# Three edits to a fused decoder layer: conditioning loads in column halves, an interleaved PSUM layout, and the order of splits at the start of the expert stage

## The chip, the cores and the metric

The kernel runs on one core of a Trainium2 chip. The metric is the device time of one execution in microseconds (us), taken on the device. The engines are named as in the profile: PE is TensorE (matmul) and PEld its weight loads, DVE is VectorE, ACT is ScalarE, POOL is GpSimd, SP is SyncE, which here only issues DMAs. Before the change three runs took 3036.16, 3039.43 and 3045.69 us; the median is 3039.43 us.

## The reference, cut to what matters

One decoder layer over 1024 tokens of width 1024, in float32. A conditioning vector gives six modulation rows; the attention half uses two kinds of heads; the second half is a retrieval layer over 128 x 128 single-neuron experts.

```python
mod = silu(c) @ ada_w + ada_b                       # 6 rows of 1024: sh1, sc1, g1, sh2, sc2, g2
h = rms_norm(x) * (1 + sc1) + sh1
...                                                 # projections, two kinds of causal attention
x = x + g1 * (mixed @ w_out)
h2 = rms_norm(x) * (1 + sc2) + sh2
s = (h2 @ w_q) . sub_keys                           # 8 heads x 2 halves x 128 scores
sv, si = top_k(s, 16)                               # per half; then the best 16 of 16 x 16 sums
g = softmax(best 16 sums); eidx = expert numbers
a = gelu(u_tab[eidx] . h2)
x = x + g2 * sum((g * a) * v_tab[eidx])
```

## The kernel before, in words

**Stages.** The program is a trunk followed by the expert stage. The trunk's order on each engine is made by a planner that simulates a timeline with costs of its own; the expert stage is in the order in which the code writes it. The trunk runs `ada(0)` (the first third of the conditioning matmul), then `project` woven with `ada_rest` (the other two thirds, `ada(1)` and `ada(2)`), then `block(0, 5)` for the first five token tiles of 128, then `block(5, 3)` for the other three woven with `route_dense`, which turns the routing of the first five tiles into dense gate matrices. `experts` then computes the first five tiles densely (all 128 x 128 experts, by two large matmuls `mm_u` and `mm_v`) and the last three by gathering rows (`gathered`), spread between the dense steps.

**`ada(g, wp)`, lines 181 to 203.** Each third has 2048 columns, four quarters of 512 that go to four 32-partition groups of one PSUM bank (`tile_position=(0, 32*q)`). For g = 0 one DMA of 1 MB brings all four quarters of a 128-row slice `k`. For g = 1 and 2 a DMA of 512 KB brings two quarters (1024 neighbouring columns, 4 KB runs), and the matmuls of these two follow; so 16 DMAs for each g, through two buffers, on the SP queue. One f32 matmul of the program is two PE instructions in the profile, each with a weight load.

**`route_dense`, `matrix(t)`, lines 870 to 907.** For every token tile 32 steps, each for four tokens: DVE compares `A` (four 128 x 128 one-hot matrices), POOL, ACT or DVE make the four `B` (by the letters in `SHARE`), PE multiplies each pair into one fourth of a bank `pg`, and ACT copies the bank into `gs` (line 904). Before the change each product has 128 neighbouring columns of PSUM, and ACT's copy writes every element 128 bytes from the one before, because `gs` has 32 tokens innermost. While `block(5, 3)` is in `attend` there is one `pg` bank, later there are two (`PG`). `A` and `B` have three buffers each, which come free when the products are done.

**`experts`, lines 1002 to 1203.** A step j of 128 does `mm_u(j)` (48 matmuls of 320 columns into the one `mm` bank pair), `gelu(j)` on ACT, `weigh(j)` on DVE, `split_c(j)` (ACT makes `CH`, DVE makes `CL`). Four steps are a group; from step 4 on, each step also runs the `mm_v` blocks of the group before, 12 matmuls each, which need the four `CH`, `CL` of that group and four units of the second table (`vh` by ACT, `vl` by DVE or POOL, in `split_v`). `mm_u(j)` needs units 2j and 2j+1 of the first table (`split_u`: `uh` on ACT, `ul` on DVE or POOL). Units below `UP` and `VP` have their second half on POOL, the others on DVE. Each split also issues the DMA of a later unit on SP. `step()` advances `gathered`: 18 routing pieces of the sixth tile on DVE, which end with its expert numbers `ei`, then a DVE dot product per gathered row; POOL issues the gathers in advance, seven buffers deep.

**The seam** is the start of `experts`. Before the change the order there is: step 0 `mm_u(0)`, `split_u(3)`, ten routing pieces, `gelu(0)`; steps 1 to 3 `mm_u(j)`, `split_u(2j+2)`, `gelu(j)`, `weigh` and `split_c` of the step before, and then `split_u(2j+3)`; in step 3 also `split_v(0)` and `split_v(1)` at the end; step 4 `mm_u(4)`, `split_c(2)`, `split_c(3)`, `split_v(2)`, `split_v(3)`, then the first `mm_v` block.

Of the kernel before, what the change touches and what calls it, by code (L numbers as in the profile page):

```python
# [43 lines left out]
UP, VP = 8, 8  # L44
# [41 lines left out]
def decoder_layer(ctx: ExitStack, tc: tile.TileContext, a, out):  # L86
# [35 lines left out]
    def tpt():  # L122
        return tp.tile([P, 4, P], FT, name="tp")
# [57 lines left out]
    def ada(g, wp):  # L181

        bt = wp.tile([P, 512], FT, name="abias", bufs=1)
        for q in range(4):
            o = a["ada_b"].offset + g * 2048 + q * 512
            (nc.gpsimd if g else nc.scalar).dma_start(bt[32 * q:32 * q + 32, :],
                                bass.AP(tensor=a["ada_b"].tensor, offset=o, ap=[[0, 32], [1, 512]]))
        ps = bank()
        n = 2 if g else 4
        for k in range(8):  # L190
            for q0 in range(0, 4, n):
                w = wp.tile([P, n, 512], FT, name="adaw")
                c = g * 2048 + q0 * 512
                (nc.sync if g or k % 2 == 0 else nc.scalar).dma_start(w, adaw[k, :, c:c + n * 512])
                for q in range(q0, q0 + n):
                    nc.tensor.matmul(ps[32 * q:32 * q + 32, :512], silb[:, k, :], w[:, q - q0, :], start=(k == 0),
                                     stop=(k == 7), skip_group_check=True, tile_position=(0, 32 * q))
        m = bt
        nc.vector.tensor_add(m, ps[:, :512], bt)
        for q in range(4 if g else 0):  # L200
            o = q * 512
            nc.gpsimd.dma_start(modd[2 * g + o // D, o % D:o % D + 512], m[32 * q:32 * q + 1, :])
        return m
# [661 lines left out]
    def route_dense(ts):  # L865

        with ExitStack() as c1:
            rp = pool(c1, "rp", 1)
            gp = pool(c1, "gp", 2)
            def matrix(t):  # L870
# [10 lines left out]
                for b in range(P // GB):  # L881
                    gs = gp.tile([P, P, GB], FT, name="gs")
                    for m0 in range(0, GB, 4):
# [17 lines left out]
                        pg = bank("pg").rearrange("p (a b) -> p a b", b=P) if "pg" in PS else tpt()  # L901
                        for o in range(4):
                            nc.tensor.matmul(pg[:, o, :], A[:, o, :], B[:, o, :], start=True, stop=True)  # L903
                        nc.scalar.activation(gs[:, :, m0:m0 + 4].rearrange("p j t -> p t j"), pg, AF.Copy)  # L904
# [97 lines left out]
    def experts():  # L1002
        with ExitStack() as c1, tc.manual_schedule():
# [42 lines left out]
            def split_v(n):  # L1046
                if n < 2 * P:
# [89 lines left out]
            for j in range(P + NJ):  # L1137
# [19 lines left out]
                if j == 0:  # L1157
                    split_u(3)
                    for _ in range(10):
                        prog[0] = next(sg)  # L1160
# [25 lines left out]
                if not blocks and live:  # L1186

# [105 lines left out]
```

## Time and profile before

| | |
|---|---|
| median of three runs | 3039.43 us |
| the profiled execution | 3038.61 us |
| its span, first to last instruction | 3036.8 us |
| mean granted TensorE clock | 0.974 of full speed |
| busy shares of the span | PE 93%, DVE 85%, POOL 47%, ACT 39% |
| trunk, up to the last copy into `gs` | 0 to 1213 us |
| seam, until the matmuls run without gaps | 1213 to 1274 us |
| dense steps | 1274 to 3037 us |

A row of the timeline has start and length in us, engine, line, operation, what is written and read, a count where neighbours are merged, and in brackets the idle time before it and what ended that. A row of a group has the count, total busy time in us and the mean of one in ns, then the engine's idle time before these instructions and what ended it. [...] The chain of work is followed back from the end; its shares say which lines lay on it in a stretch, and "issue" is time for which it names no cause.

### The profile page before, as it was taken

The page shows a single profiled execution, that of the slowest core. Times are in us where ns is not written, and L with a number is a line of the kernel's source. Part 1 is how long each engine was busy: PE and PEld are TensorE (multiplying, and loading weights), DVE is VectorE, ACT ScalarE, POOL GpSimd, SP SyncE. Part 2 cuts the span into 40 slices and gives each one's busy share as a digit, 9 for nine tenths or more (in the row PEclk, how much of TensorE's full clock was granted, in tenths as well). Part 3 has the DMA queues.
Part 4 walks back from the last instruction along what each step waited for, and adds up shares of the span by engine and source line. Part 5 has one row for each costly group of instructions (what it writes and reads, how often), then busy time and mean ns, then how long its engine had stood idle before and what let it go on. Part 6 is the DMA issues. An engine that isn't in the chain of part 4 may idle for free.

```text
span 3036.8 us, 46727 instructions
## 1 busy us (share of the span) xinstructions
PE 2837.1 (93%) x16323; PEld 2526.6 (83%) x16323; DVE 2570.6 (85%) x5380; ACT 1185.2 (39%) x2371; POOL 1418.7 (47%) x1194
## 2 busy tenths in 40 slices
PE   5999989897888799699999999999999999999998
PEld 3678777796776698699999999999989989998887
DVE  3767366599988899788888999999999999989997
ACT  4554375242886898222322222222222222222221
POOL 1121000000669974343444655566656666655761
PEclk9999999998999899899999999999999999999999
DMA  7664464721445664678798999899999999998995
GB/s 269 201 190 123 134 199 148 277 64 56 126 129 180 210 206 140 224 263 276 255 321 310 321 332 327 319 351 368 361 351 365 358 371 359 361 373 312 365 366 200
DMA packets 375564, 794.22 MB, mean 262 GB/s; under 512 B 31392, under 2 KB 171040, under 8 KB 368672
## 3 DMA queue, kind: packets, MB, share of 16 engines
q0 software_dynamic: 114400, 417.15, 38.3%
q1 hardware_dynamic: 153344, 312.48, 29.5%
q10 hardware_dynamic: 107584, 61.61, 6.9%
q8 instruction: 128, 2.10, 0.3%
q14 instruction: 108, 0.88, 0.1%
HBM read 707.74 MB, written 83.38 MB: 261 GB/s over the span
## 4 chain that ended last, share of the span: by engine, by line
PE 49%; DVE 18%; issue 12%; POOL 7%; DMA 6%; ACT 4%; SPq 0%; DVEq 0%; POOLq 0%; ACTq 0%
PE mm L1063 14%; PE pj L288 4%; PE pj L289 4%; PE pj L290 4%; POOL gath L954 4%; DVE yr L987 4%; DVE gath L974 3%; PE pg L903 3%; PE tp L289 2%; PE tp L290 2%; PE tp L288 2%; POOL B L892 2%; PE acc L288 1%; PE acc L289 1%; PE acc L290 1%
## 5 line engine op out<-in xcount | busy, mean ns | idle before, releaser
L1063 PE MATMUL mm<-h2d,uh 128*128 128x320 f32 x4096 | 770.6, 310 | 10.2 <-ACT C L1070 5.1
L954 POOL DMA_INDIRECT gath<-in_peer_u,ei x384 | 485.5, 1264 | 405.3 <-DVE gath L974 269.4
L1063 PEld LDWEIGHTS mm<-h2d,uh 128*128 128x128 f32 x4096 | 649.7, 189 | 21.1 <-ACT C L1070 6.2
L954 POOL DMA_INDIRECT gath<-in_peer_v,ef x384 | 514.9, 1341 | 307.2 <-DVE yr L987 168.7
L987 DVE SCALAR_TENSOR_TENSOR yr<-gath,co,yr 128x1024 f32<-128x1024 f32 x381 | 487.5, 1280 | 5.5 <-DMA gath<-in_peer_v,ef 1.1
L974 DVE SCALAR_TENSOR_TENSOR gath<-gath,h 128x1024 f32<-128x1024 f32 x384 | 462.7, 1221 | 26.0 <-DMA h<-h2d 13.4
L1063 PE MATMUL mm<-h2d,ul 128*128 128x320 f32 x2048 | 471.2, 311 | 12.9 <-DVE ul L279 12.4
L1070 ACT ACTIVATE C<-mm 128x640 f32<-128x640 f32 x128 | 90.5, 707 | 864.1 <-PE mm L1063 859.0
L892 POOL TENSOR_SCALAR B<-iota,T 128x128 f32<-128x128 f32 x240 | 265.6, 1115 | 266.5 <-DVE T L877 200.7
L1063 PEld LDWEIGHTS mm<-h2d,ul 128*128 128x128 f32 x2048 | 343.0, 188 | 18.3 <-DVE ul L279 17.9
L289 PE MATMUL tp<-vl,CH 128*128 128x512 f32 x600 | 235.6, 393 | 14.8 <-POOL vl L279 11.7
L903 PE MATMUL pg<-B,A 128*128 128x128 f32 x1280 | 197.2, 298 | 48.2 <-POOL B L892 26.8
L278 ACT ACTIVATE vh<-vr 128x512 fp32r<-128x512 f32 x256 | 152.9, 622 | 224.0 <-PE tp L290 145.5
L288 PE MATMUL tp<-vh,CH 128*128 128x512 f32 x600 | 234.6, 391 | 0.0
L290 PE MATMUL tp<-vh,CL 128*128 128x512 f32 x600 | 234.1, 390 | 0.0
L903 PEld LDWEIGHTS pg<-B,A 128*128 128x128 f32 x1280 | 174.9, 206 | 69.0 <-POOL B L892 39.3
L904 ACT ACTIVATE gs<-pg 128x512 f32<-128x512 f32 x160 | 173.8, 1087 | 56.7 <-PE pg L903 56.2
L278 ACT ACTIVATE uh<-ur 128x512 fp32r<-128x512 f32 x256 | 155.4, 619 | 74.8 <-DMA ur<-in_u_t 67.7
L279 DVE TENSOR_TENSOR ul<-ur,uh 128x512 fp32r<-128x512 f32 x248 | 173.6, 700 | 0.0
L279 DVE TENSOR_TENSOR vl<-vr,vh 128x512 fp32r<-128x512 f32 x248 | 160.0, 682 | 7.2 <-ACT vh L278 7.0
L1074 DVE TENSOR_TENSOR C<-C,G 128x640 f32<-128x640 f32 x128 | 105.2, 823 | 55.0 <-ACT C L1070 54.9
L288 PE MATMUL acc<-vh,CH 128*128 128x512 f32 x384 | 149.8, 390 | 0.0
(321 smaller groups left out, 5978.9 us busy)
## 6 DMA issues: line engine op xcount, KB each, us to landing
ur<-in_u_t SPq DMA_DIRECT2D x256, 256.0 KB, 6.3
vr<-in_peer_v SPq DMA_DIRECT2D x256, 256.0 KB, 6.9
gd<-gs ACTq DMA_DIRECT2D x20, 2048.0 KB, 9.3
G<-gd SPq DMA_DIRECT2D x32, 1280.0 KB, 8.8
adaw<-in_ada_w SPq DMA_DIRECT2D x32, 512.0 KB, 4.3
wraw<-in_peer_w_q SPq DMA_DIRECT2D x128, 128.0 KB, 2.7
wraw<-in_w_out SPq DMA_DIRECT2D x32, 256.0 KB, 3.6
wraw<-in_w_in SPq DMA_DIRECT2D x24, 256.0 KB, 3.8
```

Of the source, the lines that this page charges most:

```text
L278: nc.scalar.activation(hi, src, AF.Copy)
L279: (eng or nc.vector).tensor_sub(lo, src, hi.bitcast(FT))
L288: nc.tensor.matmul(out, ah, bh, start=start, stop=False)
L289: nc.tensor.matmul(out, ah, bl, start=False, stop=False)
L290: nc.tensor.matmul(out, al, bh, start=False, stop=stop)
L892: nc.gpsimd.tensor_scalar(B[:, m, :], iota128, T[:, 1, c + m:c + m + 1], T[:, 2, c + m:c + m + 1], op0=OP.is_equal, op1=OP.mult)
L903: nc.tensor.matmul(pg[:, o, :], A[:, o, :], B[:, o, :], start=True, stop=True)
L904: nc.scalar.activation(gs[:, :, m0:m0 + 4].rearrange("p j t -> p t j"), pg, AF.Copy)
L954: nc.gpsimd.indirect_dma_start(out=u, out_offset=None, in_=tab, in_offset=bass.IndirectOffsetOnAxis(ap=idx, axis=0))
L974: nc.vector.scalar_tensor_tensor(got[n], got[n], 1.0, q["h2"], op0=OP.mult, op1=OP.mult, accum_out=q["dots"][:, s:s + 1])
L987: nc.vector.scalar_tensor_tensor(yr, v, q["co"][:, s:s + 1], yr, op0=OP.mult, op1=OP.add)
L1063: nc.tensor.matmul(ps[:, o, 0:C2], s[:, k % 4, :], h2[:, mv, k, o * C2:(o + 1) * C2], start=st, stop=(k == 7 and s is l))
```

## The change

`ada`: for g = 1 and 2 a DMA brings half of the columns (256) of all four quarters in place of all columns of two quarters; the size stays 512 KB and the runs become 1 KB. The eight matmuls of a half have 256 columns; each half has a bank of its own and an addition of its own. `matrix`: the product of token o goes to every fourth column of the bank, so that the four tokens lie side by side; ACT's copy then reads the bank in order and writes runs of four neighbouring elements. `experts`: `split_u(2j+3)` of steps 0 to 3 stands directly behind `gelu(j)`, ahead of `weigh` and `split_c`; `split_v(0)` to `split_v(3)` stand behind it in steps 1 and 2 (their later calls find nothing to do); with `VP` at 0 DVE makes `vl` of the first eight units in place of POOL.

```diff
--- before.py
+++ after.py
@@ -41,7 +41,7 @@
 AHEAD = 2
 PG = 2
 LAGV = 2
-UP, VP = 8, 8
+UP, VP = 8, 0
 
 UR, VR = 3, 4
 
@@ -185,18 +185,20 @@
             o = a["ada_b"].offset + g * 2048 + q * 512
             (nc.gpsimd if g else nc.scalar).dma_start(bt[32 * q:32 * q + 32, :],
                                 bass.AP(tensor=a["ada_b"].tensor, offset=o, ap=[[0, 32], [1, 512]]))
-        ps = bank()
-        n = 2 if g else 4
+
+        H = 256 if g else 512
+        pss = [bank() for _ in range(0, 512, H)]
         for k in range(8):
-            for q0 in range(0, 4, n):
-                w = wp.tile([P, n, 512], FT, name="adaw")
-                c = g * 2048 + q0 * 512
-                (nc.sync if g or k % 2 == 0 else nc.scalar).dma_start(w, adaw[k, :, c:c + n * 512])
-                for q in range(q0, q0 + n):
-                    nc.tensor.matmul(ps[32 * q:32 * q + 32, :512], silb[:, k, :], w[:, q - q0, :], start=(k == 0),
-                                     stop=(k == 7), skip_group_check=True, tile_position=(0, 32 * q))
+            for h0 in range(0, 512, H):
+                w = wp.tile([P, 4, H], FT, name="adaw")
+                src = adaw[k, :, g * 2048:(g + 1) * 2048].rearrange("p (q n) -> p q n", n=512)[:, :, h0:h0 + H]
+                (nc.sync if g or k % 2 == 0 else nc.scalar).dma_start(w, src)
+                for q in range(4):
+                    nc.tensor.matmul(pss[h0 // H][32 * q:32 * q + 32, :H], silb[:, k, :], w[:, q, :],
+                                     start=(k == 0), stop=(k == 7), skip_group_check=True, tile_position=(0, 32 * q))
         m = bt
-        nc.vector.tensor_add(m, ps[:, :512], bt)
+        for i, ps in enumerate(pss):
+            nc.vector.tensor_add(m[:, i * H:(i + 1) * H], ps[:, :H], bt[:, i * H:(i + 1) * H])
         for q in range(4 if g else 0):
             o = q * 512
             nc.gpsimd.dma_start(modd[2 * g + o // D, o % D:o % D + 512], m[32 * q:32 * q + 1, :])
@@ -898,10 +900,12 @@
                             else:
                                 nc.vector.tensor_scalar(B[:, m, :], iota128, T[:, 1, c + m:c + m + 1],
                                                         T[:, 2, c + m:c + m + 1], op0=OP.is_equal, op1=OP.mult)
-                        pg = bank("pg").rearrange("p (a b) -> p a b", b=P) if "pg" in PS else tpt()
+
+                        pg = (bank("pg") if "pg" in PS else tpt().rearrange("p a b -> p (a b)")).rearrange(
+                            "p (j t) -> p j t", t=4)
                         for o in range(4):
-                            nc.tensor.matmul(pg[:, o, :], A[:, o, :], B[:, o, :], start=True, stop=True)
-                        nc.scalar.activation(gs[:, :, m0:m0 + 4].rearrange("p j t -> p t j"), pg, AF.Copy)
+                            nc.tensor.matmul(pg[:, :, o], A[:, o, :], B[:, o, :], start=True, stop=True)
+                        nc.scalar.activation(gs[:, :, m0:m0 + 4], pg, AF.Copy)
                         yield 1.2
                     nc.scalar.dma_start(gd[:, :, t * (P // GB) + b].rearrange("p a j t -> p a (j t)"),
                                       gs.rearrange("p (a j) t -> p a (j t)", j=NJ))
@@ -1044,7 +1048,7 @@
                     nc.sync.dma_start(vr[n], vtab[j, :, c * 512:(c + 1) * 512])
 
             def split_v(n):
-                if n < 2 * P:
+                if n in vr:
                     vs[n] = (vp.tile([P, 512], FR, name="vh"), vp.tile([P, 512], FR, name="vl"))
                     split(vr.pop(n), *vs[n], nc.gpsimd if n < VP else None)
                     load_v(n + VR)
@@ -1155,7 +1159,6 @@
                 if live:
                     ps = mm_u(j)
                 if j == 0:
-                    split_u(3)
                     for _ in range(10):
                         prog[0] = next(sg)
                 while pend:
@@ -1184,6 +1187,10 @@
                     pend.append((*blk, pv))
                     step()
                 if not blocks and live:
+                    split_u(2 * j + 3)
+                    if 0 < j < 3:
+                        split_v(2 * j - 2)
+                        split_v(2 * j - 1)
 
                     for i in (j - 1, j) if j == NJ - 1 else (j - 1,):
                         if i >= 0:
```

## Rows read from the trace of the kernel before

**Rows 1.** Windows: busy us of each engine in five stretches of the span.
```profile
50.00:100.00 50.00, 50.00 (x264) 34.34 (x264) 32.59 (x84) 31.57 (x81) 1.51 (x2) 1.00 0.71 227
...
764.00:918.00 154.00, 131.62 (x925) 119.95 (x924) 134.27 (x355) 128.95 (x247) 104.27 (x95) 0.90 0.40 119
918.00:1060.00 142.00, 112.66 (x635) 95.01 (x633) 122.58 (x269) 106.60 (x199) 142.00 (x121) 0.90 0.63 197
1060.00:1213.00 153.00, 142.30 (x993) 135.55 (x991) 149.12 (x584) 132.47 (x288) 98.19 (x108) 0.99 0.59 178
...
1300.00:1700.00 400.00, 400.00 (x2254) 365.67 (x2254) 336.98 (x592) 104.13 (x175) 181.13 (x146) 1.00 0.84 288
```

**Rows 2.** Timeline of PE: conditioning matmuls, four quarters at once, then two.
```profile
31.66 5.38 PE L196 MATMUL pj<-adaw,silb 128*32 128x512 f32 x32 [1.31 <-DMA adaw<-in_ada_w]
...
99.59 1.05 PE L196 MATMUL pj<-adaw,silb 128*32 128x512 f32 x4
```

**Rows 3.** The chain of work from 38 to 215 us, shares by line.
```profile
by line: PE pj L288 8.9%; PE pj L289 8.3%; PE pj L290 8.2%; DMA wraw<-in_w_in 7.3%; DMA qd<-stage 5.5%; PE pj L196 3.9%; DMA adaw<-in_ada_w 3.6%; PE tp L452 2.2%; DVE wl L279 1.1%; issue 1.0%; ACT hf L367 0.9%; ACT wh L278 0.9%; DVE stage L
```

**Rows 4.** DMA issues, 40 to 200 us, and two queues of the whole span (packets, MB, share of 16 engines).
```profile
adaw<-in_ada_w SPq DMA_DIRECT2D x30, 512.0 KB, 4.3
...
q1 hardware_dynamic: 153344, 312.48, 29.5%
q10 hardware_dynamic: 107584, 61.61, 6.9%
```

**Rows 5.** Groups of instructions by form, 764 to 1213 us.
```profile
L903 PE MATMUL pg<-B,A 128*128 128x128 f32 x1280 | 197.2, 298 | 48.2 <-POOL B L892 26.8 <-issue 11.8 <-ACT gs L904 2.7
...
L904 ACT ACTIVATE gs<-pg 128x512 f32<-128x512 f32 x160 | 173.8, 1087 | 56.7 <-PE pg L903 56.2 <-ACT sc L782 0.2
...
L593 ACT ACTIVATE pT<-tp 128x512 f32<-128x512 f32 x25 | 15.0, 603 | 0.0
```

**Rows 6.** Timeline around one gate product, 830 to 835 us.
```profile
830.46 1.06 ACT L904 ACTIVATE gs<-pg 128x512 f32<-128x512 f32 x1 [1.50 <-PE pg L903]
...
831.62 2.05 PE L903 MATMUL pg<-B,A 128*128 128x128 f32 x8 [1.19 <-issue]
```

**Rows 7.** The chain of work, by line: 764 to 918, 918 to 1060, 1060 to 1213 us.
```profile
by line: PE pg L903 25.1%; PE mm L580 14.3%; issue 10.5%; PE ov L659 9.6%; POOL B L892 7.5%; ACT gs L904 6.6%; PE tp L592 3.7%; ACT pT L593 3.0%; ACT p L564 2.5%; ACT L564 2.5%; ACT B L896 2.3%; ACT pd L564 2.2%; ACT B L895 1.8%; ACT L229 1
...
by line: POOL B L892 36.7%; issue 15.3%; PE pg L903 11.3%; PE pj L289 7.4%; POOL wl L279 7.2%; PE pj L290 6.6%; PE pj L288 6.1%; ACT gs L904 1.6%; ACT B L895 1.4%; ACT B L896 1.2%; ACT L846 0.9%; PE tp L739 0.6%; DVE fp L792 0.5%; ACT wh L2
...
by line: DVE B L899 20.5%; DVE A L887 16.8%; PE pg L903 14.3%; DVE si L792 5.9%; DVE top L793 5.1%; DVE sv L791 4.6%; DVE si L795 4.5%; PE pj L290 4.1%; PE mm L1063 3.9%; PE pj L288 3.8%; PE pj L289 3.7%; DVE sv L794 3.4%; ACT gs L904 2.7%;
```

**Rows 8.** Timeline of PE at full clock: one gate product, four contiguous passes.
```profile
849.89 1.11 PE L903 MATMUL pg<-B,A 128*128 128x128 f32 x8
...
1219.85 0.74 PE L1063 MATMUL mm<-h2d,uh 128*128 128x320 f32 x4
```

**Rows 9.** Timeline of PE in the seam: its longest wait.
```profile
1261.62 0.39 PE L288 MATMUL tp<-vh,CH 128*128 128x512 f32 x1
1273.71 0.80 PE L289 MATMUL tp<-vl,CH 128*128 128x512 f32 x1 [11.70 <-POOL vl L279]
```

**Rows 10.** Timeline of DVE in the seam.
```profile
1242.17 0.83 DVE L279 TENSOR_TENSOR CL<-C,CH 128x640 fp32r<-128x640 f32 x1 [2.92 <-ACT CH L278]
...
1247.25 0.69 DVE L841 TENSOR_TENSOR oh<-oh,sf 128x1024 bf16<-128x1024 bf16 x1
...
1252.05 1.77 DVE L841 TENSOR_TENSOR oh<-oh,sf 128x1024 bf16<-128x1024 bf16 x1
...
1267.43 1.22 DVE L974 SCALAR_TENSOR_TENSOR gath<-gath,h 128x1024 f32<-128x1024 f32 x1 [8.45 <-DMA gath<-in_peer_u,ei]
...
1269.85 1.55 DVE L279 TENSOR_TENSOR CL<-C,CH 128x640 fp32r<-128x640 f32 x2
```

**Rows 11.** Timeline of POOL in the seam.
```profile
1250.20 3.07 POOL L279 TENSOR_TENSOR vl<-vr,vh 128x512 fp32r<-128x512 f32 x2 [6.05 <-ACT vh L278]
...
1272.23 3.11 POOL L279 TENSOR_TENSOR vl<-vr,vh 128x512 fp32r<-128x512 f32 x2
```

## The prediction

> **What bounds the kernel now.** I read the windows first, to see which engine is full in which stretch; then the chain of work in the stretches that the change touches; then the groups by form for the durations; and the timeline only where a wait has to be seen. The dense steps are PE's alone: from 1300 to 1700 us PE is busy for all 400 us [rows 1]. No edit changes their matmuls, so what the change wins or loses is how much earlier or later PE enters them. Before them there are four regimes. From 50 to 100 us PE is full [rows 1]. From 764 to 918 us, where the gate products run beside attention with one bank, no engine is full: PE, DVE and ACT are busy for 132, 134 and 129 of 154 us [rows 1], and the chain passes through PE, "issue" and ACT [rows 7]. From 918 to 1060 us POOL is busy for all 142 us, from 1060 to 1213 us DVE for 149 of 153 [rows 1]. The seam ends with PE waiting 11.70 us for a `vl` on POOL [rows 9].
>
> **Part 1, conditioning.** DMAs, bytes and additions' columns stay; each g has one more addition and one more bank. What changes is PE's time. Two quarters of 512 columns take four instructions, 1.05 us. With all four quarters at hand 32 instructions took 5.38 us, 1.34 for eight: four quarters cost little more than two, so they run side by side [rows 2]. Eight instructions of 256 columns should therefore take about half of 1.34, 0.67 us, and a DMA's worth of work falls by 0.38. That is 32 x 0.38 = 12 us of PE. How much is on the path? The first 16 run where PE is full; for them 16 x 0.38 = 6 us count. Of the whole stretch the chain names 3.9% of 177 us, 6.9 us, for these matmuls [rows 3]; by that alone 6.9 x 0.38 / 1.05 = 2.5 us. So 2.5 to 12; I take 6.5, the full first half and little of the second. Against it stand the shorter runs. Queue 10 moved 61.61 MB in 107584 packets, 573 B each, at 6.9% of 16 engines; queue 1 moved 2038 B each, 312.48 MB at 29.5% [rows 4]: 18.4 against 21.8 KB per engine and us. So 1 KB runs cost at most 19% more. The chain has 3.6% of 177 us, 6.4 us, on these DMAs [rows 3], so up to 1.2 us. The second bank leaves project four of six; I cost it at nothing, because PE is full with the work of the other five [rows 1]; if it isn't covered, it takes from this part's gain. **Sum -5.5 us** (between -1 and -12).
>
> **Part 2, the gate products.** The copy into `gs` takes 1087 ns; a copy of as many elements from PSUM that writes them in order takes 603 [rows 5]. Its price is bounded by these two rows; a loss has no reason, since it reads as before and writes longer runs. I take 603, the nearer in form: four neighbours, then a step. So 0.48 us each, 160 times, 77 us of ACT. Most of that is not on the path. It counts where the copy is waited for. With one bank the next product waits for the copy: the copy from 830.46 to 831.52 us ends just ahead of the product at 831.62, whose wait the profile calls "issue", 1.19 us [rows 6]; there are five such pieces of 1.19 to 1.20 us on the chain between 764 and 918 us, 6.0 us. The copy itself is 6.6% of 154 us there, 10.2 us, then 1.6% of 142 and 2.7% of 153, 6.4 us [rows 7]. Together 22.6 us, of which 45% go: 10 us. POOL, full from 918 us on, will take back some; I take **-8 us** (between 0, if POOL or DVE is late next everywhere, and -22, which is 0.48 for each of the 46 copies between 764 and 918 us).
>
> The other side is PE's strided write. No matmul of the trace writes PSUM with a step. At full clock a gate product's eight instructions take 1.11 us [rows 8], of which the last one's own length is about 0.30 [rows 5]: 0.116 us apart, 0.9 ns per column. The contiguous passes of 320 columns stand 0.14 us apart (0.74 less about 0.31 for the last, over three), 0.45 ns per column [rows 8]. So PSUM takes columns in order at twice the rate at which the gate products deliver them; a write up to twice as slow is hidden. The bounds are no cost and a product twice as long; I take none, because of that factor.
>
> [...]
>
> **Part 3, the seam.** Removed: PE's wait for the third `vl`, which POOL starts at 1272.23 us behind its gathers [rows 11]. But what is late next is close. The first block also needs `CL(2)`, and DVE makes that from 1269.85 us [rows 10], the first of the two ready at about 1270.6; DVE stood before it for a gathered row, 8.45 us, which followed the expert numbers. So 1273.71 can fall to 1270.6 at once, and further only if DVE gets to the expert numbers earlier. On DVE four `vl` come ahead of them: `CL` of 640 columns takes 0.83 [rows 10], so 0.7 for 512 columns, +2.8 us. `CL(1)` waited 2.92 us for ACT [rows 10], because `uh(5)` stood behind `CH(0)` and made `mm_u(2)`, and with it `gelu(2)`, late; now `uh(5)` is ahead, and one hand-over of 0.8 stays: -2.1. POOL's two `vl` at 1250.20 us [rows 11] go: a DVE multiplication beside them took 1.77 us, the same one alone 0.69 [rows 10]; that and the `ul` beside them give back 2.1. Net -1.4 (between that and +2.8). So `CL(2)` is ready at about 1269.2 (to 1273.4), and PE resumes there: -4.5 to -0.3, **taken -4 us**. Everything that PE wins earlier in the seam only lengthens this wait. The moved splits also issue loads of `ur` and `vr` earlier on SP, behind the same loads as before; nobody waits for them. The four later `vl` on DVE lie beside full PE work, where DVE is busy for 337 of 400 us [rows 1]: nothing.
>
> **Sum.** 3038.6 (the profiled execution, of which 1.8 lies outside its span; 0.8 under the median) - 5.5 - 8 - 4 = **3021 us**, 0.6% less. All parts are in series, so each arrives at the end unless the planner orders the trunk otherwise. The parts' bounds give 3000 to 3037.
>
> **The rivals.** First, *only the seam arrives*: POOL and DVE set the pace of the gate stage whatever ACT does (POOL full for 142 us speaks for it, the gaps on all engines before 918 us against it), or the copy stays at 1087 ns, so that the edit doesn't do what it says; the conditioning gives its -1. Then -1 - 0 - 4: 3033 us. Second, slower: *the strided write doubles the gate products*. Its place is 764 to 1213 us, where they are 25.1%, 11.3% and 14.3% of the chain [rows 7], 38.7 + 16.0 + 21.9 = 76.6 us, on an engine with only 22 + 29 + 11 us free [rows 1]. It decides once a column takes more than the 0.9 ns of now, and at twice that the time is 3021 + 77 = 3098 us. For it speaks that no row shows such a write at any price; against it the factor of two that the products leave unused.
>
> **Chances.** The forecast 0.62, only the seam 0.19, doubled products 0.19. A measurement of this kernel tells about 0.3% (9 us) from no change: faster means under 3030, slower over 3048. Nearly all of the forecast and a quarter of the first rival lie under 3030: faster 0.64; the rest of both 0.17; slower 0.19. The range runs from 3000, the best of the bounds, to 3048; it leaves out the second rival. The forecast's own range is 3000 to 3037.
>
> **What would show it.** Right: conditioning matmuls eight in about 0.7 us; the copy near 600 ns; the gate products still eight in 1.1 us at full clock; PE's longest wait in the seam 8 to 10 us and ended by `CL`. Wrong: the copy still over 1 us; products over 1.5 us at full clock; or a trunk whose last copy into `gs` is no earlier than 1213 us minus a few, which would say that POOL or DVE took the gain back.

## The result: 32 us less, and the profile after

The median of four runs is 3009.95 us after (3006.18 to 3012.80) and 3042.07 us before (3036.16 to 3045.69): a ratio of 0.9896, with 95% between 0.9875 and 0.9917. The profiled execution took 3010.34 us with a span of 3008.5, against 3038.61 and 3036.8 before. The direction and the places were as forecast; the size was not: 28 us between the two profiles, 32 between the medians, where the sum had 17.5.

The page after, first the busy time of the engines, then one row of the DMA issues. PE has 17 us less to do than before (2837.1), ACT 52 less (1185.2), POOL 12 less (1418.7), DVE 4 less (2570.6).

```profile
PE 2819.9 (94%) x16451; PEld 2525.3 (84%) x16451; DVE 2566.3 (85%) x5390; ACT 1133.6 (38%) x2371; POOL 1406.5 (47%) x1186
...
adaw<-in_ada_w SPq DMA_DIRECT2D x32, 512.0 KB, 5.0
```

The windows of after, with the columns of [rows 1]: for a stretch of the span the length, the busy time and count of PE, PEld, DVE, ACT and POOL, the granted clock (1.00 is full speed), the DMA share and GB/s. The first three are its gate stage (one bank; POOL full; DVE full), the next its seam, the last the same dense stretch as in [rows 1].

```profile
763.00:899.00 136.00, 120.47 (x905) 108.51 (x904) 130.75 (x348) 113.61 (x250) 103.67 (x93) 0.99 0.45 129
899.00:1049.00 150.00, 118.66 (x647) 100.37 (x647) 129.30 (x312) 87.55 (x195) 145.45 (x126) 0.89 0.66 211
1049.00:1195.00 146.00, 136.23 (x963) 130.88 (x962) 141.62 (x554) 108.64 (x281) 92.15 (x101) 0.99 0.56 161
1196.00:1248.00 52.00, 36.40 (x202) 34.54 (x203) 42.08 (x113) 15.82 (x24) 15.04 (x13) 0.84 0.67 227
1300.00:1700.00 400.00, 400.00 (x2254) 365.65 (x2253) 341.61 (x595) 104.90 (x176) 185.44 (x146) 1.00 0.84 291
```

PE is busy for all 400 us of the dense stretch, before and after, with the same 2254 instructions: what is won is an earlier entry, as the prediction said. The first window holds as many PE instructions in its 136 us (905) as the kernel before has in 152 (902, from 768 to 920 us), and there the granted clock is 0.99 where before has 0.90.

Where the two traces part, as the start of the same piece of work after minus before, each from the first instruction of its trace:

| point | after minus before, us |
|---|---|
| last conditioning matmul | -6.0 |
| first copy into `gs` | -4.3 |
| 47th copy (the first behind the one-bank stretch) | -21.4 |
| 96th copy (the first behind POOL's stretch) | -12.1 |
| last, 160th copy | -16.9 |
| `gelu(6)` to `gelu(32)` | -26.7 |
| `gelu(64)` | -26.5 |
| end | -28.3 |

So some 4 us come before the gate stage, some 17 inside its first stretch, of which POOL's stretch takes 9 back and DVE's gives 5 again, some 10 in the seam, and 1.6 in the dense steps.

Groups by form in the gate stage of after, to set beside [rows 5]: the products are no slower, and the copy has fallen from 1087 to 592 ns.

```profile
L907 PE MATMUL pg<-B,A 128*128 128x128 f32 x1280 | 188.7, 291 | 38.6 <-POOL B L894 20.9 <-issue 4.3 <-ACT B L898 3.4
...
L908 ACT ACTIVATE gs<-pg 128x512 f32<-128x512 f32 x160 | 94.7, 592 | 72.1 <-PE pg L907 71.8
```

PE's conditioning matmuls of after, eight to a DMA, to set beside [rows 2]. Eight take 0.64 us at full clock (behind the wait of 2.64 us the granted clock is 0.50 from 102.0 to 103.1 us, and eight take 1.08).

```profile
95.37 0.64 PE L197 MATMUL pj<-adaw,silb 128*32 128x256 f32 x8
98.07 0.64 PE L197 MATMUL pj<-adaw,silb 128*32 128x256 f32 x8 [0.95 <-DMA adaw<-in_ada_w]
102.01 1.08 PE L197 MATMUL pj<-adaw,silb 128*32 128x256 f32 x8 [2.64 <-DMA adaw<-in_ada_w]
```

PE's two waits in the last part of the seam of after, to set beside [rows 9]; behind the second PE runs on without a gap.

```profile
1231.62 0.90 PE L1067 MATMUL mm<-h2d,ul 128*128 128x320 f32 x2 [4.97 <-DVE ul L281]
...
1247.04 0.80 PE L292 MATMUL tp<-vh,CL 128*128 128x512 f32 x1 [5.43 <-DVE CL L281]
```

### The profile page after: what moved, and what is told of

Same layout as the page of the kernel before. It is cut to its first block, busy times and chain, and to the rows that moved or that the text cites. A ratio compares the mean times of both kernels' runs of the same rounds, so it can differ in the third digit from the quotient of the medians.

```text
span 3008.5 us, 46963 instructions
## 1 busy us (share of the span) xinstructions
PE 2819.9 (94%) x16451; PEld 2525.3 (84%) x16451; DVE 2566.3 (85%) x5390; ACT 1133.6 (38%) x2371; POOL 1406.5 (47%) x1186
## 4 chain that ended last, share of the span: by engine, by line
PE 58%; DVE 18%; issue 10%; DMA 7%; POOL 4%; ACT 4%; SPq 0%; DVEq 0%; ACTq 0%; POOLq 0%
PE mm L1067 18%; PE pj L290 5%; PE pj L291 5%; PE pj L292 4%; DVE yr L991 4%; PE tp L291 3%; PE tp L292 3%; PE tp L290 3%; PE acc L290 2%; PE acc L292 2%; PE acc L291 2%; POOL gath L958 2%; DVE gath L978 2%; DVE B L901 1%; DVE A L889 1%
## 5 line engine op out<-in xcount | busy, mean ns | idle before, releaser
L1067 PEld LDWEIGHTS mm<-h2d,uh 128*128 128x128 f32 x4096 | 651.1, 189 | 16.9 <-ACT C L1074 7.3
L907 PE MATMUL pg<-B,A 128*128 128x128 f32 x1280 | 188.7, 291 | 38.6 <-POOL B L894 20.9
L291 PE MATMUL acc<-vl,CH 128*128 128x512 f32 x384 | 149.9, 390 | 0.0
```

Of the source, the lines that this page charges most:

```text
L291: nc.tensor.matmul(out, ah, bl, start=False, stop=False)
L907: nc.tensor.matmul(pg[:, :, o], A[:, o, :], B[:, o, :], start=True, stop=True)
L1067: nc.tensor.matmul(ps[:, o, 0:C2], s[:, k % 4, :], h2[:, mv, k, o * C2:(o + 1) * C2], start=st, stop=(k == 7 and s is l))
```

## The experiments

Theory: the three parts are in series, the stepped PSUM write costs nothing, and what arrives is PE's shorter conditioning, the shorter copy, and a seam that ends on `CL`. Rivals: one part brings nearly all (the seam alone, or the copy alone); the stepped write costs something that the copy hides; of the seam, the engine of `vl` does it and not the order. All ratios are to the kernel before on the same chip, with 95% intervals; at 3040 us, 0.001 is 3 us. A kernel with an interval has between 4 and 12 runs; two kernels were run once, and their texts say so. Differences between traces are taken as in the table above.

**One part alone.** First the conditioning:

```diff
-            for q0 in range(0, 4, n):
-                w = wp.tile([P, n, 512], FT, name="adaw")
+            for h0 in range(0, 512, H):
+                w = wp.tile([P, 4, H], FT, name="adaw")
...
+            nc.vector.tensor_add(m[:, i * H:(i + 1) * H], ps[:, :H], bt[:, i * H:(i + 1) * H])
```

> Only the conditioning edit. The changed kernel came out 28 us shorter in its profile: its last conditioning matmul stood 6 us earlier, its first copy into gs 4 us earlier, the last copy 17 us earlier. Theory 'in series': each edit wins in its own stretch, so this one alone gives 4 to 6 us, all before 200 us, and the gate stage (764 to 1213 us) stays as long as before. Rival 'other order': the edit makes the planner order the whole trunk anew, and part of the shorter gate stage is owed to that; then this alone gives 8 us or more and its gate stage is shorter although the copies still take 1.09 us.

Measured: 3031.06 us, 0.9969 (0.9955 to 0.9983), some 9 us less. In its trace the last conditioning matmul is only 2.5 us earlier and the first copy into `gs` 3.2; the last copy is 1.8 earlier, the dense steps 7.2. So half of the part's gain does not lie in its own stretch; where it lies is told below, with the conditioning.

Second the PSUM layout:

```diff
-                            nc.tensor.matmul(pg[:, o, :], A[:, o, :], B[:, o, :], start=True, stop=True)
-                        nc.scalar.activation(gs[:, :, m0:m0 + 4].rearrange("p j t -> p t j"), pg, AF.Copy)
+                            nc.tensor.matmul(pg[:, :, o], A[:, o, :], B[:, o, :], start=True, stop=True)
+                        nc.scalar.activation(gs[:, :, m0:m0 + 4], pg, AF.Copy)
```

> Only the interleaved PSUM layout; the order of the instructions is that of before on every engine. Theory 'the copy pays': copies at about 0.6 us, products still eight in 1.1 us at full clock, the stretch from the first to the last copy 10 to 13 us shorter, total 10 to 13 us. Rival 'other order': that stretch shrinks by 5 us or less without the conditioning edit's new order. Rival 'POOL keeps the pace': the stretch from 918 to 1060 us takes back what the one before won, total under 4 us.

Measured: 3026.10 us, 0.9950 (0.9936 to 0.9965), some 15 us less, the largest of the three. Every engine has its instructions in the order of before, so this trace is the cleanest to compare: 16.0 us earlier at the 47th copy, 12.7 at the 96th, 12.4 at the last, 13.0 at the end. POOL's stretch takes 3 back.

Third the seam:

```diff
-UP, VP = 8, 8
+UP, VP = 8, 0
...
-                    split_u(3)
...
+                    split_u(2 * j + 3)
+                    if 0 < j < 3:
+                        split_v(2 * j - 2)
+                        split_v(2 * j - 1)
```

> Only the seam's edit, trunk as before. Theory 'PE waits for CL': PE resumes the first block 4 to 5 us earlier, right behind CL(2), not behind a vl; the time from the expert numbers to the first gathered row stays near 8 us, total 4 to 5 us. Rival 'the seam alone is worth 8 to 10': the expert numbers come 3 us earlier, and the first gathered row lands 2 us sooner because fewer loads run beside it; then 8 us or more.

Measured: 3029.87 us, 0.9972 (0.9957 to 0.9987), some 8.5 us less; from the start of the last copy to that of `gelu(6)` its trace has 81.9 us where before has 90.4, also 8.5. That is the rival of its expectation, not the theory. (Its one profile was 6 us earlier in the trunk as well, where it changes nothing; runs of before on that chip lie between 3029.92 and 3048.72 us, and what differs in this profile is the clock, see below.)

The three parts alone add up to -0.31 - 0.50 - 0.28 = -1.09%, and together they measure -1.04%. So "only the seam arrives" is out, and the totals add as far as the intervals tell. Place by place they don't. Up to the last copy the parts' traces give 1.8 + 12.4 us (the seam's trunk left out) and the change has 16.9; from there to `gelu(6)` they give 5.4 + 0.5 + 8.5 = 14.4 us and the change 9.8. In the seam two parts win the same microseconds in part, as told below.

**The stepped write with the old copy.** PE writes every fourth column, but ACT still reads token by token, so that its writes stay 128 bytes apart.

```diff
-                            nc.tensor.matmul(pg[:, o, :], A[:, o, :], B[:, o, :], start=True, stop=True)
-                        nc.scalar.activation(gs[:, :, m0:m0 + 4].rearrange("p j t -> p t j"), pg, AF.Copy)
+                            nc.tensor.matmul(pg[:, :, o], A[:, o, :], B[:, o, :], start=True, stop=True)
+                        nc.scalar.activation(gs[:, :, m0:m0 + 4].rearrange("p j t -> p t j"),
+                                             pg.rearrange("p j t -> p t j"), AF.Copy)
```

> The kernel before, with the products written to every fourth PSUM column, and a copy that still goes token by token: it reads with a step of 16 bytes and writes with one of 128. It holds PE's strided write without the copy's gain. Theory 'the strided write is hidden': products eight in 1.1 us at full clock, copies at 1.05 to 1.1 us, total within 4 us of before. Rival 'the write costs, and the copy's gain covered it': products over 1.2 us for eight, total 5 us or more over before.

Measured: 3040.50 us, 0.9992 (0.9979 to 1.0004): no difference. Its groups by form, 764 to 1213 us:

```profile
L904 PE MATMUL pg<-B,A 128*128 128x128 f32 x1278 | 195.9, 299 | 50.0 <-POOL B L892 25.7 <-issue 13.2 <-ACT gs L905 4.0
...
L905 ACT ACTIVATE gs<-pg 128x512 f32<-128x512 f32 x160 | 173.4, 1085 | 59.0 <-PE pg L904 58.8 <-ACT sc L782 0.2
```

The product takes 299 ns and the copy 1085, against 298 and 1087 in [rows 5]. The stepped write is free here, the stepped read of PSUM adds nothing to ACT's scattered copy either, and the whole price of the old copy (1087 ns, where the change has 592) was its scattered write. The second rival (doubled products) is out.

**How far the write is from being the limit.** After the kernel's work, 40 matmuls of 512 columns each, in eight bursts: in bf16 and then in f32, each in order, to every fourth column, to every second, and in order again. The tail's results are used by nothing.

```diff
+            for kind, w, m in (("b", wb[:, 0:P], mb[:, 0:512]), ("f", ident, mv[:, 0:512])):
+                for t in (1, 4, 2, 1):
...
+                    o = pr.rearrange("p (j t) -> p t j", t=t) if t > 1 else pr
+                    for _ in range(40):
+                        nc.tensor.matmul(o, w, m.rearrange("p (t j) -> p t j", t=t) if t > 1 else m,
+                                         start=True, stop=True)
```

> The changed kernel with a tail of eight bursts of 40 matmuls of 512 columns behind the last block, whose results are not used: bf16 then f32, each with columns in order, every fourth, every second, in order. It prices the step of the write by itself; the tail adds about 100 to 200 us. Theory 'hidden by f32's half rate': bf16 in order about 0.22 us apart, stepped bf16 up to 0.43; f32 the same stepped or not (an f32 product is two instructions of about 0.43). Rival 'a stepped write costs nothing at all': bf16 stays at 0.22 too. Rival 'it costs f32 as well': f32 stepped over 0.5.

Measured in its one run (timeline of PE; one f32 matmul is two instructions):

```profile
3013.91 10.48 PE L1220 MATMUL pj<-gath,ident 128*128 128x512 bf16 x40 [3.31 <-DVE gath L1212]
3025.17 17.33 PE L1220 MATMUL pj<-gath,ident 128*128 128x512 bf16 x40 [0.78 <-DVE gath L1222]
3043.28 17.33 PE L1220 MATMUL pj<-gath,ident 128*128 128x512 bf16 x40 [0.78 <-DVE gath L1222]
3061.39 8.79 PE L1220 MATMUL pj<-gath,ident 128*128 128x512 bf16 x40 [0.78 <-DVE gath L1222]
3070.97 34.60 PE L1220 MATMUL pj<-gath,ident 128*128 128x512 f32 x80 [0.78 <-DVE gath L1222]
3106.35 34.60 PE L1220 MATMUL pj<-gath,ident 128*128 128x512 f32 x80 [0.78 <-DVE gath L1222]
...
3177.11 34.60 PE L1220 MATMUL pj<-gath,ident 128*128 128x512 f32 x80 [0.78 <-DVE gath L1222]
```

In order, a bf16 matmul of 512 columns takes 0.22 us (8.79 / 40; in the first burst, of 10.48, the granted clock is 0.50 from 3014.3 to 3017.7 us, while all the others ran at 1.00); stepped, by two or by four columns alike, 0.43 (17.33 / 40): 1.97 times as long. In f32 each instruction takes 0.43 us (34.60 / 80) in every layout. So the stepped write took a bf16 matmul from 0.22 to 0.43 us, and an f32 instruction takes those 0.43 us in order already. Reading the step off [rows 8] as "0.9 ns per column against 0.45" was right, and the factor of two that it left was used up whole. By these numbers the same layout under bf16 products would have been the second rival; no run here has such products.

**Two neighbours instead of four.** Products go to every second column, two tokens side by side, so that the copy writes runs of 8 bytes.

```diff
-                            nc.tensor.matmul(pg[:, o, :], A[:, o, :], B[:, o, :], start=True, stop=True)
+                            nc.tensor.matmul(pg[:, o // 2, :, o % 2], A[:, o, :], B[:, o, :], start=True, stop=True)
```

> The kernel before with two tokens side by side in place of four: products to every second PSUM column, the copy writes runs of 8 bytes. It separates what makes the copy slow. If it is the number of separate runs, each costing the same, the copy goes half of the way, about 0.84 us; if two neighbours are enough, about 0.6; if only runs of 16 bytes are fast, it stays at 1.08. The total would be 6 to 13 us under before in the middle case.

Measured: one run of 3030.39 us beside a median of 3042.06 before. The copies (count, then min, median and max in ns, first and last start):

```profile
L905 ACT ACTIVATE gs<-pg x160: 577/624/671, 772.3 to 1203.6; 128x512 f32<-128x512 f32 x160
```

A median of 624 ns with two neighbours, 597 with four, 1081 with none: the second neighbour does nearly all of it.

**The seam, order against engine.** The new kernel with POOL making the first `vl` again, and the new kernel with the old order but `vl` on DVE:

```diff
-UP, VP = 8, 0
+UP, VP = 8, 8
```

> The changed kernel, with vl of the first eight units back on POOL but in the new order. Theory 'the order wins, not the engine': the first four vl stand ahead of POOL's gathers now, so no wait for a vl before the first block; DVE is spared 2.8 us ahead of the expert numbers but slowed beside POOL; total within 3 us of the changed kernel. Rival 'POOL was the cause': the later four vl, behind gathers, hold PE again; a wait of 3 us or more ended by a vl on POOL between the first block and the sixth step, total 3 to 10 us over the changed kernel.

```diff
...
+                    split_u(3)
...
-                    split_u(2 * j + 3)
-                    if 0 < j < 3:
-                        split_v(2 * j - 2)
-                        split_v(2 * j - 1)
```

> The changed kernel with the old order of the seam, but vl on DVE as in the change. Theory 'the order wins': DVE again stands about 3 us for CH(1), because gelu(2) is late, so the expert numbers come 2 to 3 us later; vl(2) follows the two CL, 1 to 2 us more; total 3 to 5 us over the changed kernel. Rival 'the engine wins': under 2 us over it.

Measured: 0.9911 (0.9895 to 0.9926) with POOL, 0.9902 (0.9887 to 0.9917) with the old order, 0.9896 for the change. The intervals overlap, so times alone don't part them; the traces do in part. From the last copy to `gelu(6)`: 80.6 us for the change, 81.4 with the old order, 83.0 with POOL, 90.4 before. The routing behind its first ten pieces, up to `ei`, takes 25.4, 25.3, 27.1 and 28.3 us. With POOL, its `vl` stand beside a comparison and a product of DVE, twice each:

```profile
1215.89 3.59 POOL L281 TENSOR_TENSOR vl<-vr,vh 128x512 fp32r<-128x512 f32 x2 [1.34 <-ACT vh L280]
...
1216.12 2.20 DVE L840 TENSOR_TENSOR oh<-abb,iota 128x1024 bf16<-128x1024 bf16 x1
1218.24 1.92 DVE L1078 TENSOR_TENSOR C<-C,G 128x640 f32<-128x640 f32 x1
```

In the change the same two stand alone:

```profile
1211.99 1.23 DVE L840 TENSOR_TENSOR oh<-abb,iota 128x1024 bf16<-128x1024 bf16 x1
...
1214.34 0.82 DVE L1078 TENSOR_TENSOR C<-C,G 128x640 f32<-128x640 f32 x1
```

That is 4.1 us more in all, for 2.4 us of `vl` that DVE is spared. The old order costs DVE in another place, the four multiplications `oh<-oh,sf`; first the old order, then the change:

```profile
1210.08 1.77 DVE L843 TENSOR_TENSOR oh<-oh,sf 128x1024 bf16<-128x1024 bf16 x1
...
1216.69 1.79 DVE L843 TENSOR_TENSOR oh<-oh,sf 128x1024 bf16<-128x1024 bf16 x1
...
1221.03 0.69 DVE L843 TENSOR_TENSOR oh<-oh,sf 128x1024 bf16<-128x1024 bf16 x1
```

```profile
1216.76 1.75 DVE L843 TENSOR_TENSOR oh<-oh,sf 128x1024 bf16<-128x1024 bf16 x1
...
1224.52 0.68 DVE L843 TENSOR_TENSOR oh<-oh,sf 128x1024 bf16<-128x1024 bf16 x1
```

In the old order two of the four are long, each beside a `ul` on POOL (from 1209.90 and 1216.51 us); in the change one is (`ul` from 1216.58 us), before three were. That is the same effect as in [rows 10]. In the old order PE has one wait of 8.73 us for `vl`, now on DVE, in the new one 4.97 for `ul` and 5.43 for `CL`, and the end is nearly the same.

So neither theory holds as it stood: with POOL no `vl` held PE again, and the old order was not 3 to 5 us slower. The kernel with the conditioning alone, which has no edit of the seam, takes 85.0 us from the last copy to `gelu(6)`. Beside that the order alone brings 2.0 us, the engine alone 3.6 and both 4.4: in these single traces the engine does more, by too little for the times to show.

**What is late next: four attempts to use the wait that is left.** If PE waits for `CL` because DVE stands before it for a gathered row, then `split_c(2)` and `split_c(3)` ahead of that row should end it:

```diff
...
+                    if j == NJ - 1 and tk[0] == 4:
+                        split_c(j - 1)
+                        split_c(j)
```

> The changed kernel, with split_c(2) and split_c(3) moved ahead of the first gathered row's dot product, into step 3 behind the 18th routing piece. If what is left of the seam's wait (5.43 us, ended by CL) is DVE standing at a gathered row with CL queued behind it, PE goes from mm_u(4) into the first block with under 1 us of waiting and the total falls by 5 to 7 us against the changed kernel, 33 to 38 us against before. If instead something else is next (units of the first table on DVE, gelu behind its table load), the gain is under 2 us.

Then with the unit that PE waits for next moved as well (units 10 and 11 of the first table earlier, 8 and 9 on POOL):

```diff
-UP, VP = 8, 0
+UP, VP = 10, 0
...
+                if j == NJ:
+                    split_u(2 * j + 3)
...
+                        split_c(j - 1)
+                        split_c(j)
+                        split_u(2 * j + 4)
```

> As the earlier run with split_c(2) and split_c(3) ahead of the gathered rows, and now also the units of the first table that PE asked for next: split_u(10) with them, split_u(11) at the start of step 4, and the ul of units 8 and 9 on POOL. In the earlier run PE's 5.43 us for CL went, and 4.97, 3.58 and 1.11 us for ul on DVE stood in its place. If those were all, PE runs from mm_u(4) through mm_u(5) with waits of under 2 us in sum and the total falls 6 to 9 us under the changed kernel. If DVE is simply behind (it has the gathered rows to do as well), the waits move to the next steps and under 3 us are left.

Then with the row tile of `h2` loaded at the start of `gathered`, because in the last one the first gathered product waited 7.31 us for it:

```diff
+        st[ts[0]]["h2"] = w.tile([P, D], FT, name="h2", bufs=1)
+        nc.sync.dma_start(st[ts[0]]["h2"], h2d[ts[0]])
...
```

> As the run with split_c, split_u(10) and split_u(11) moved ahead, and the row tile that the gathered products multiply is loaded at the start of the stage, not behind the seam's splits on SP. In that run PE was 7 us ahead of the changed kernel at gelu(5) and had lost all of it at gelu(6); its first gathered product waited 7.31 us for that row tile. If the stretch behind the seam is set by the stream of gathered products on DVE, which starts with the first of them, an earlier start is kept to the end: the first product 2 to 4 us earlier, the total 2 to 4 us under the changed kernel. If the gathers themselves are the limit, the first product then waits for them and under 1 us is won.

And then with the gathered products of the sixth tile spread thinner, so that fewer stand ahead of `ul` on DVE:

```diff
-PACE = (1.3, 1.05, 1.5)
+PACE = (1.6, 1.05, 1.5)
```

> As early_row, with the first tile's gathered products spread thinner over the steps (1.6 for 1.3 each in the pace). Theory 'the stream on DVE sets the steps behind the seam': with fewer products per step PE keeps its lead of about 7 us past gelu(6), total 5 to 9 us under the changed kernel; the products left over are done in the last third, where DVE is fuller, which can take some back. Rival: PE's lead is lost again within three steps, so what holds it is not the number of products.

Measured: 0.9908 (0.9887 to 0.9929), 0.9913 (0.9896 to 0.9931), 0.9906 (0.9885 to 0.9928) and 1.0001 (0.9989 to 1.0013). The first three do what they say and gain nothing over the change; the fourth loses all of it. PE's last waits with `early_c_and_u`:

```profile
1250.07 0.56 PE L1067 MATMUL mm<-h2d,ul 128*128 128x320 f32 x2 [2.00 <-DVE ul L281]
1265.80 0.85 PE L1067 MATMUL mm<-h2d,uh 128*128 128x320 f32 x4 [0.83 <-ACT uh L280]
1271.28 0.90 PE L1067 MATMUL mm<-h2d,ul 128*128 128x320 f32 x2 [4.63 <-DVE ul L281]
```

At `gelu(5)` PE is 32.7 us ahead of before, 6 more than with the change; at `gelu(6)` it is 25.6 ahead, and the lead is gone, because `ul` stands on DVE behind gathered products (this row at 1271.28; 4.64 us at the same place with `early_row`). Starting the gathered products earlier does not mend that: with `early_row` the first of them stands 48.2 us behind the last copy in place of 51.8, and `gelu(6)` 81.3 in place of 81.4. Fewer of them per step do: with the thinner spread `gelu(6)` stands 77.5 us behind the last copy, where the change has 80.6, and PE is 29.1 us ahead of before up to `gelu(32)`. So when PE enters its gapless run is set by how much DVE has to do there, gathered products above all, and not by `CL` as such: the row of [rows 9] and its successor name only the last piece of it. But the spread moves the work to a stretch where DVE has little to spare. The windows of `early_row_pace`:

```profile
1300.00:1700.00 400.00, 399.55 (x2250) 364.93 (x2249) 311.29 (x539) 104.90 (x176) 150.07 (x124) 1.00 0.77 263
2200.00:2700.00 500.00, 483.10 (x2687) 437.33 (x2686) 470.10 (x646) 122.50 (x207) 323.25 (x250) 1.00 0.97 361
```

and the second stretch in the change:

```profile
2200.00:2700.00 500.00, 499.61 (x2810) 456.13 (x2809) 480.43 (x657) 129.11 (x218) 330.03 (x249) 1.00 0.99 367
```

DVE does 30 us less in the first stretch than the change's 341.61, and PE then stands idle for 16.9 of 500 us in the second, where the change was idle for 0.4; at the end the kernel stands 6.3 us behind before. None of the four beats the changed kernel.

## Why the prediction was right, and where its sizes were off

**Where and in which direction.** Its signs came, but for the length of one: conditioning matmuls eight in 0.64 us (0.67 forecast), the copy at 592 ns (603), products unchanged, PE's last wait of the seam ended by `CL` (5.43 us, where 8 to 10 was forecast), the last copy into `gs` at 1194.9 us in place of 1211.8. The bounds' sum of 3000 to 3037 held 3010.

**The sum.** Each part alone measured more than its term: 9 us against 5.5, 15 against 8, 8.5 against 4. For the gate products the interval (11 to 20 us) leaves the term out; for the other two (5 to 14, 4 to 13) it just reaches it, so there the profiles have to carry the argument.

**The gate term failed on the clock.** I costed the stretch of 764 to 918 us as issue pieces and copies, 16.2 us times 45%, 7.3 us. It fell by 16 to 17. The windows show why. Before, in three of the pieces of low clock in that stretch and one between them:

```profile
779.30:786.10 6.80, 5.61 (x27) 5.22 (x26) 4.96 (x12) 4.14 (x9) 4.73 (x4) 0.50 0.00 0
786.10:827.10 41.00, 38.11 (x289) 34.51 (x287) 39.14 (x95) 35.23 (x70) 26.15 (x24) 1.00 0.48 148
827.10:840.80 13.70, 9.66 (x41) 8.69 (x41) 7.34 (x17) 8.96 (x15) 10.54 (x9) 0.50 0.29 80
...
885.10:891.90 6.80, 5.62 (x27) 5.22 (x27) 5.35 (x11) 3.99 (x8) 3.89 (x4) 0.50 0.00 0
```

For 27.3 us here, and 3.4 more at 912, the granted clock is 0.50, and PE's 41 instructions from 827 to 841 take 9.66 us. [rows 6] lies inside that piece: the product at 831.62 took 2.05 us, where [rows 8] has 1.11, and I read its wait and not its length. Four of the five pieces of 1.19 us that the sum took (from 780.50, 827.19, 830.42 and 833.66 us) lie in stretches with a granted clock of 0.50. The same stretch, from the first to the 47th copy, before and in the single-part kernels: first before, then the seam alone (old copy), then the layout alone, then the stepped write with the old copy:

```profile
768.00:920.00 152.00, 129.15 (x902) 117.41 (x901) 131.97 (x346) 126.95 (x245) 102.27 (x95) 0.90 0.39 118
```

```profile
767.00:912.00 145.00, 120.27 (x903) 108.53 (x901) 131.41 (x347) 126.17 (x245) 100.02 (x93) 0.99 0.41 123
```

```profile
768.00:903.00 135.00, 119.39 (x898) 107.36 (x898) 129.77 (x344) 110.70 (x243) 100.11 (x90) 0.99 0.44 132
```

```profile
766.00:918.00 152.00, 128.34 (x904) 116.27 (x902) 131.79 (x347) 126.70 (x245) 100.67 (x94) 0.91 0.39 118
```

The seam-only kernel has the trunk of before and the old copy; only the clock stayed up, and the stretch takes 144.7 us in place of 151.4. The layout alone takes 135.5. So at the same clock the copies are worth 9.2 us (7.3 forecast: about right), and the low clock another 6.7, for which the sum had no term. These are single traces. Whether the copy causes the low clock is open: all ten traces with the short copy show 0.99 in this stretch, the four with the old one 0.90, 0.91, 0.92 and 0.99. So the low clock was seen only with the old copy, but not always, and other gaps than the copy's stood ahead of it too. Just before the fall at 827 PE had waited for a `B` of POOL:

```profile
826.06 1.13 PE L903 MATMUL pg<-B,A 128*128 128x128 f32 x8 [2.00 <-POOL B L892]
```

The give-back was forecast in kind ("POOL will take back some") and is 3.2 us with the order of before. The 9 us that the change gives back in POOL's stretch are mostly the conditioning's: alone it loses 6.9 there and wins 4.2 in the next.

**The stepped write.** No row stood behind the second rival's doubled product; the doubling was my assumption. Measured, the stepped write took bf16 matmuls of 512 columns from 0.22 to 0.43 us each and left the f32 products of this kernel as they were (299 against 298 ns). Weighing it by the rate at which the products deliver columns gave the right answer. For the copy I had taken the 603 ns of another copy from PSUM; measured, it took 592 ns with four neighbours and 624 with two, against 1087 with none.

**Conditioning.** PE's saving per DMA was right, but on its stretch only 2.5 to 6 us came, because the loads became late next. The chain from 38 to 208 us of the change:

```profile
by line: issue 24.3%; PE pj L290 12.2%; PE pj L291 11.0%; PE pj L292 10.7%; DMA adaw<-in_ada_w 9.8%; PE pj L197 8.5%; DMA wraw<-in_w_in 3.2%; PE tp L364 3.2%; PE tp L454 3.1%; PE tp L398 1.5%; ACT hf L369 1.4%; POOL kd L440 1.4%; POOL kd L4
```

The loads of `adaw` have 9.8% of 170 us, 16.7 us, where [rows 3] has 6.4 us; single pieces of it are 5.55 and 5.89 us long, and the median landing went from 4.3 [rows 4] to 5.0 us. From 38 to 200 us PE's matmuls waited 6.5 us for these loads in place of 0.8 (7.2 with this part alone). I had costed the short runs at 1.2 us.

What made up for it I had only named as an exception, "unless the planner orders the trunk otherwise"; that it came out as a gain is luck as far as the forecast goes. With this part the instructions of the trunk stand in another order, from 48 us on. The routing of the sixth tile then begins 0.3 us behind the start of the last copy in place of 3.1, and behind its first ten pieces takes 26.2 us in place of 28.3; from the last copy to `gelu(6)` this kernel has 85.0 us without any edit of the seam, where before has 90.4. The 28.3 fell to 26.2 because DVE's second `CL` waits 0.85 us where [rows 10] has 2.92:

```profile
1235.49 0.83 DVE L281 TENSOR_TENSOR CL<-C,CH 128x640 fp32r<-128x640 f32 x1 [0.85 <-ACT CH L280]
```

That is the wait for which the prediction gave the seam's new order 2.1 us. The seam alone ends it too (0.80 us), so together the two parts win it once: here the parts are not in series. That all this comes with the conditioning's new order of the trunk is shown; that it would do so again for another edit of the conditioning isn't.

**The seam.** The mechanism was right, the piece was too small. The timeline of DVE in the change:

```profile
1223.78 0.82 DVE L281 TENSOR_TENSOR CL<-C,CH 128x640 fp32r<-128x640 f32 x1 [0.81 <-ACT CH L280]
...
1237.03 0.28 DVE L860 SCALAR_TENSOR_TENSOR ei<-e 128x128 int32<-128x128 f32 x1
1243.70 1.23 DVE L978 SCALAR_TENSOR_TENSOR gath<-gath,h 128x1024 f32<-128x1024 f32 x1 [6.38 <-DMA gath<-in_peer_u,ei]
...
1246.16 1.56 DVE L281 TENSOR_TENSOR CL<-C,CH 128x640 fp32r<-128x640 f32 x2
```

PE resumes at 1247.04, as soon as the first `CL` is there, as forecast. I took 3.1 us for going from `vl` to `CL`, and 1.4 net for DVE reaching `ei` earlier. The first came, 2.9: PE resumes 3.34 us behind the start of the first gathered product in place of 6.28. Of the second there is more. The net was +2.8 for four `vl`, -2.1 for the wait of `CL` and -2.1 for what POOL's splits had slowed; in the routing up to `ei` these measure +2.4, -2.0 and -3.3 (two multiplications less at 1.77 us are 2.2 of it, one `ul` the rest), 2.9 us in sum. Another 2.1 come between `ei` and the first gathered product, which waits 6.38 us in place of 8.45 [rows 10]; for these the sum had no term, and no run here shows what shortened that wait. All three are 7.9. In the whole change the seam is some 9.8 us shorter: these 7.9, and 2.8 from the routing's earlier begin, which is the conditioning's, less 1.0 by which the first ten pieces grew. And since 2.0 of the 7.9 come with the conditioning too, the seam's edit is worth less beside it than alone: the step from 85.0 us with the conditioning alone to 80.6 with everything is 4.4, about the term of 4; no run has those two parts alone. And "PE's longest wait 8 to 10 us" was 5.43, with another 4.97 now before it, for `ul`.

## What to carry to other kernels

A copy that scatters single elements can be mended at its source (here it fell from 1087 to 592 ns), if the matmuls that fill the bank deliver columns no faster than a stepped write takes them; measure that rate first, since here an f32 instruction of 512 columns took 0.43 us in every layout, where a bf16 one went from 0.22 to 0.43. When a wait is removed in a stretch where the engine already starves, price the work in that stretch at the clock that its rows show, not only the wait: over 40% of that stretch's gain (6.7 of 16 us) went with pieces that no longer ran at a granted clock of 0.50, though what keeps the clock up stays open. And ahead of a wait that ends a start-up phase, ask which engine's work sets the entry into the full stretch: moving the named piece alone gave back its lead within one step. When parts add up in total, check them place by place as well: here two of them ended the same wait.

## What the runs showed of the hardware that was not expected

A stepped PSUM write cost the same at a step of two and of four columns (17.33 us for 40 bf16 matmuls of 512 columns, 8.79 in order), and nothing at all in f32 (34.60 us for 80 instructions in each layout). ACT's copy of 128 x 512 f32 from PSUM took 1087 ns with single elements written 128 bytes apart (1085 when it also read PSUM with a step), 624 with two neighbours and 592 with four. A load of 512 KB took 5.0 us from issue to landing in runs of 1 KB and 4.3 in runs of 4 KB (medians); with this small difference, two buffers and a PE that had become quicker, 16.7 us of these loads lay on the chain in place of 6.4.
